# A one-core decoder layer: the order of weight loads, Silu, lambdas and banks, and a gate kept in SBUF

## The chip, the cores and the metric

The kernel runs on one core of a Trainium2 chip. The core has five engines that run side by side: TensorE (PE in the profile) multiplies matrices into PSUM, VectorE (DVE) and ScalarE (ACT) do elementwise work and are the ones that empty PSUM, GpSimd (POOL) does elementwise work in SBUF only, and SyncE (SP) does nothing but issue DMA transfers. ScalarE and GpSimd also issue a few. Each engine takes its instructions strictly in the order in which the program wrote them; between engines there are semaphores. The metric is device time in microseconds (us), less is better.

## The reference, cut to what matters

One layer, 512 tokens, width 1024, all in 32-bit floats:

```python
h = x @ w_in                                   # 1024 -> 9 x 1024
ua, va, za, qh, kh, vh, zb, ga, gb = split(h)
ya = gelu(ua) * spatial(layer_norm(gelu(va))) * silu(za)      # spatial: 8 groups, 128x128 lower triangular
lam = exp(sum(lam_q1 * lam_k1)) - exp(sum(lam_q2 * lam_k2)) + 0.2
o = diff_attention(rope(qh) / 8, rope(kh), vh, lam)           # 8 heads, 2 maps of 64, causal
yb = rms_norm(o) * 0.8 * silu(zb)
merged = sigmoid(ga) * (ya @ w_branch_a) + sigmoid(gb) * (yb @ w_branch_b)
ple = sigmoid(x @ w_ple_gate) * (p @ w_ple)                   # p: 512 x 256
x = layer_norm(2 ** 0.25 * x + merged @ w_out + ple)
```

The embedding's gate is `sigmoid(x @ w_ple_gate)`, called `pg` below; the lambdas are the scalars of `lam`.

## The kernel before

**Products.** Every fp32 matrix is split into a high part that TensorE reads in one pass (`wh`, made by a ScalarE copy) and a low part (`wl`, the rest, made by a VectorE subtraction). One matmul of the reference becomes three (`three`): high by high, high by low, low by high. Each of these 128x512 matmuls is a *product*, and `product` counts them. The count is the kernel's clock: `later(n, fn)` puts `fn` on an agenda, and it is written into the program as soon as n more products have been written. So "at product 14 of a unit" is a place in the program order of every engine that `fn` uses, not a time. The matmuls of attention and of the spatial products are not counted.

**Weights.** The weights are cut into units of 128x1024 (512 KB). `load(u)` has SP fetch unit u into one of three buffers `wr`; the buffer that unit u+3 needs is that of unit u, free once u is split. `spread(u)` writes the split: the high part two products later, the low part twelve. `next_unit` is called when TensorE starts unit u: it writes the loads up to u+5 and the split of u+3. A unit of q, k, zb, ua or za is 24 products long.

**Stages, in order.** 1. v from x (192 products, eight PSUM banks, `values_of_x`); the rope tables and `lam` are made on the side. While k, q and zb of the first head pair run, sums of quarters of x are made and stored (`sums_of_x`, issued from ScalarE). 2. Four rounds, one for each pair of heads p: `rope("k", p)`, `rope("q", p)`, `gate_b(p)`, each of two units. `rope` turns the banks with the tables, splits the result and has SP stack it by small copies (`stack`, L528; in round 0 half of them go by POOL), 24 products after the group; for k a pair of swapped copies per head follows 10 and 20 products later (`swap`, L539). `gate_b` has ScalarE empty two banks with Silu into `yb` (L560), `GATE` products after their last one. Attention of pair p-1 (`attention`) is spread over round p: its first score matmuls (L575) come at product 14 of the round. VectorE empties them (L580), ScalarE takes exponentials (L586), VectorE combines the two maps, TensorE transposes (L610), ScalarE copies them out (L612), TensorE multiplies by v (L621). There are three PSUM banks `pp` in turn for the units, two `sc` for scores, and `tr`, `po`, `tx`. 3. The rest of ua, and za. 4. Four `quad` stages, va, ga, gb, pg (x by w_ple_gate), 168 products each: a fast matrix product with seven products of quarters instead of eight. Weights of some steps are made by adding one unit onto another with an accumulating DMA from POOL (`follow`, L249). `keep` (L794) copies a bank out on ScalarE, `block` (L799) joins two pieces on VectorE, and `done` finishes a block 128x512. For ga, gb and pg `done` is `gate_done`: Sigmoid on ScalarE into a scratch tile (tag `t`, six buffers), and a store to DRAM by SP (L900). The spatial products (L875) read va and run in gb and in the first 40 products of pg. 5. `ple`: two units, 24 products each, p by w_ple into four banks each; `embed` (L935) multiplies each bank on VectorE by the gate, fetched from DRAM by `load_gate`, into `base`. 6. wb and wa (192 products each), out, and the last layer norm, which uses `lg` and `lb`.

PSUM sets for stages of eight banks are `main_banks()` (three `pp` and `tx`) and `other_banks()` (two `sc`, `tr`, `po`). wb writes the other banks first:

```python
    for c in range(2):
        banks = main_banks() if c else other_banks()
```

A tile with a tag takes the memory of the tile that had the tag before; the first write waits for the last use of the old one. `va`, and later `base`, have the tag V.

Of the kernel before, what the change touches and what calls it, by code (L numbers as in the profile page):

```python
# [12 lines left out]
F32 = mybir.dt.float32  # L13
# [3 lines left out]
AF = mybir.ActivationFunctionType  # L17
OP = mybir.AluOpType
AX = mybir.AxisListType

P = 128
D = 1024
T = 512
KT = D // P
NT = T // P
# [8 lines left out]


WARM = 9
GATE = 1
HIGH = (2,)
LOW = (12,)
ROPE = (2, 6, 8, 14, 18, 24)  # L40
# [121 lines left out]
def bcast(ap, n, parts=P):  # L162
    return bass.AP(tensor=ap.tensor, offset=ap.offset, ap=[[0, parts], [1, n]])
# [3 lines left out]
def hybrid_layer(ctx: ExitStack, tc: tile.TileContext, a, out: bass.AP):  # L167
    nc = tc.nc
    pe, dve, act, pool, sp = nc.tensor, nc.vector, nc.scalar, nc.gpsimd, nc.sync
# [7 lines left out]
    dram = ctx.enter_context(tc.tile_pool(name="dram", bufs=1, space=bass.MemoryType.DRAM))  # L177

    def pbank(tag, bufs):
        return psum.tile([P, T], F32, tag=tag, name=f"ps_{tag}", bufs=bufs)  # L180

    def pp():
        return pbank("pp", 3)

    def main_banks():
        return [pp(), pp(), pp(), pbank("tx", 1)]

    def other_banks():
        return [pbank("sc", 2), pbank("sc", 2), pbank("tr", 1), pbank("po", 1)]
# [5 lines left out]
    def later(n, fn, *args):  # L195

        clock[1] += 1
        heapq.heappush(agenda, (clock[0] + n, clock[1], fn, args))
# [30 lines left out]
    def load(u, pieces=1):  # L229
        if u >= len(STEPS) or u in raw or STEPS[u][3] is not None:  # L230
            return
        _, unit, chain, _ = STEPS[u]
        if chain == "a":
            if not sums:
                return
            r = sums[0].tile([P, 1024], F32, name="wa", tag="wa", bufs=3)
        else:
            r = wraw.tile([P, 1024], F32, name="wr", tag="wr")
        n = 1024 // pieces
        raw[u] = r  # L240
        for j in range(pieces):
            sp.dma_start(out=r[:, j * n:(j + 1) * n], in_=W[unit][:, j * n:(j + 1) * n])
            yield

    def follow(u):

        if u in FOLLOWS:
            raw[FOLLOWS[u]] = raw[u]
            pool.dma_start(out=raw[u], in_=W[STEPS[FOLLOWS[u]][1]], accum_op=OP.add)  # L249

    def parts_of(u):
        h = wsp.tile([P, 1024], F32R, name="wh", tag="wh")
        l = wsp.tile([P, 1024], F32R, name="wl", tag="wl")
        split[u] = (h, l)
        return h, l

    def prep(u, pieces=1):
        if u < len(STEPS) and u not in split:
            run(load(u))
            h, l = parts_of(u)  # L260
            n = 1024 // pieces
            for j in range(pieces):
                s = slice(j * n, (j + 1) * n)
                cut(h[:, s], l[:, s], raw[u][:, s])
                yield
            follow(u)

    def spread(u, high=HIGH[0], low=LOW[0]):

        if u >= len(STEPS) or u in split:  # L270
            return
        h, l = parts_of(u)

        def high_part():
            act.activation(h, raw[u], AF.Copy)  # L275

        def low_part():
            dve.tensor_tensor(out=l, in0=raw[u], in1=h.bitcast(F32), op=OP.subtract)  # L278
            follow(u)

        later(high, high_part)
        later(low, low_part)

    def next_unit(name):
        u = cursor[0]
        assert STEPS[u][0] == name, (STEPS[u][0], name)
        cursor[0] += 1
        for g in (prep(u), prep(u + 1), prep(u + 2), load(u + 3), load(u + 4), load(u + 5)):
            run(g)
        spread(u + 3)  # L290
        return split.pop(u)

    def next_pair(name):
# [21 lines left out]
    def run(gen):  # L315
        for _ in gen:
            pass

    def feature_group(ps, name, mh, ml):
        h, l = next_unit(name)  # L320
        for k in range(KT):
            s = slice(k * P, (k + 1) * P)
            three(ps, h[:, s], l[:, s], mh[:, k, :], ml[:, k, :], k == 0, k == KT - 1)
# [28 lines left out]
    for k in range(KT):  # L352
# [3 lines left out]
        if k < 2:  # L356
# [9 lines left out]
                       base=0, pattern=[[-1, P]], channel_multiplier=1)  # L366
# [186 lines left out]
    def gate_b(p):  # L553
# [7 lines left out]

        later(GATE, out_of)

# [112 lines left out]
                later(n + d, fn, h)  # L676

    rope_tables()
    later(150, lam)
    values_of_x()  # L680
    sums_of_x()
    ua = big.tile([P, KT, T], F32, name="ua", tag="U")
# [47 lines left out]
    post = ctx.enter_context(tc.tile_pool(name="post", bufs=1))  # L730
    sums.append(post)

    def tmp(name):
        return post.tile([P, T], F32, name=name, tag="t", bufs=6)
# [49 lines left out]
    def quad(name, turn, place, done, last=None):  # L784


        pair = [pp(), pp()], [pp(), pbank("tx", 1)]
        X, Y = pair if turn else pair[::-1]
        Z = [pbank("sc", 2) for _ in range(2)]
        kept = {}  # L790

        def keep(key, bank):
            kept[key] = tmp(key[0])
            act.activation(kept[key], bank, AF.Copy)  # L794

        def block(c, t, first, second, op, spare):
            z = place(c, t)
            z = spare if z is None else z
            dve.tensor_tensor(out=z, in0=first, in1=second, op=op)  # L799
            later(2, done, c, t, z, z)  # L800

        def after1(t):
            keep(("s1", t), Y[t])

        def after2(t):
            s1 = kept.pop(("s1", t))
            block(0, t, X[t], s1, OP.add, s1)

        def after5(t):
            keep(("s5", t), Z[t])  # L810

        def after6(t):
            keep(("s2", t), Y[t])
            later(2, block_of_6, t)

        def block_of_6(t):
            s2 = kept.pop(("s2", t))
            block(1, t, Z[t], s2, OP.subtract, s2)

        def after7(t):  # L820
            s5 = kept.pop(("s5", t))
            block(1, 2 + t, s5, Y[t], OP.subtract, s5)

        def after4(t):
            z = place(0, 2 + t)
            done(0, 2 + t, tmp("z") if z is None else z, Y[t])

        steps = ((X11, Y, True, after1), (X12, X, True, after2), (XS1, Z, True, after5),
                 (XN4, Z, False, None), (XS2, Y, False, after6), (XS3, Y, False, after7),
                 (X22, Y, False, after4))  # L830
        for i, (x, bank, first, after) in enumerate(steps):
            w = next_pair(name)
            if i == 6 and last:
                last()
            for t in range(2):
                for k in range(4):
                    h, l = w[k // 2]
                    m = slice((k % 2) * T, (k % 2 + 1) * T)
                    three(bank[t], *x(t, k), h[:, m], l[:, m], first and k == 0, k == 3, True)
                if after:  # L840
                    later(1, after, t)
# [50 lines left out]
        later(SPATIAL[0] + SPATIAL[1] * g, spatial, g)  # L892


    gates = {n: dram.tile([NT, 2, P, T], F32, name=f"gate_{n}") for n in ("ga", "gb", "pg")}

    def gate_done(name):
        def done(c, t, z, source):
            act.activation(z, source, AF.Sigmoid)
            sp.dma_start(out=gates[name][t, c], in_=z)  # L900

        return done
# [18 lines left out]
            later(40 + 12 * k, cut, phl[0][:, 0, k, :], phl[0][:, 1, k, :], pt)  # L921

    later(64, load_p)
    quad("pg", False, lambda c, t: None, gate_done("pg"), begin_ya)


    base = post.tile([P, NT, D], F32, name="base", tag="V")
    gate = {}

    def load_gate(name, c, t):  # L930
        gate[name, c, t] = tmp("gate")
        sp.dma_start(out=gate[name, c, t], in_=gates[name][t, c])

    def embed(c, t, bank):
        dve.tensor_tensor(out=base[:, t, c * T:(c + 1) * T], in0=bank, in1=gate.pop(("pg", c, t)), op=OP.mult)  # L935

    def residue(c, t):
        z = base[:, t, c * T:(c + 1) * T]
# [8 lines left out]
    def cut_yb(g):  # L947
        cut(ybh[:, g, :], ybl[:, g, :], yb[:, g, :])

    banks = other_banks(), main_banks()  # L950
    for t in range(NT):
        load_gate("pg", 1, t)
    for g in range(KT):
        later(4 + 12 * g, cut_yb, g)
    for c in (1, 0):
        h, l = next_unit("ple")
        for t in range(NT):
            ts = slice(t * P, (t + 1) * P)
            for k in range(2):
                m = slice(k * T, (k + 1) * T)  # L960
                three(banks[c][t], phl[0][:, 0, k, ts], phl[0][:, 1, k, ts], h[:, m], l[:, m], k == 0, k == 1)
            later(1, embed, c, t, banks[c][t])
            if c:
                later(4, load_gate, "pg", 0, t)


    lg = post.tile([P, D], F32, name="lg", tag="g")
    lb = post.tile([P, D], F32, name="lb", tag="b")
    pool.dma_start(out=lg, in_=bcast(a["ln_g"], D))
    pool.dma_start(out=lb, in_=bcast(a["ln_b"], D))  # L970

    mb = big.tile([P, NT, D], F32, name="mb", tag="Y")

# [7 lines left out]
    for c in range(2):  # L981
        banks = main_banks() if c else other_banks()
# [25 lines left out]
    for c in range(2):  # L1008
        banks = main_banks() if c else other_banks()
# [37 lines left out]
    banks = other_banks()  # L1047
# [4 lines left out]
    for t in range(NT):  # L1052
        ts = slice(t * P, (t + 1) * P)
        n = T if t < NT - 1 else T // 2
        for j in range(T // n):
            bank = pp()
# [50 lines left out]
```

## Time and profile before

| | us |
|---|---|
| median of 3 runs | 651.64 (651.27 to 652.54) |
| profiled execution, its own time | 649.57 |
| span of its trace, first to last instruction | 647.9 |
| TensorE busy in it | 629.4 |
| VectorE, ScalarE, GpSimd busy | 411.2, 298.8, 135.7 |
| DMA moved | 112.62 MB |

The granted clock of TensorE is 0.996 of full speed over the span. In the profile, L with a number is a line of the kernel. A row of the timeline is: start, length, engine, line, operation, what it writes and reads, shapes, how many in a row were merged (x4), and in brackets the idle time before it and what ended that. A `q` behind an engine's name is its sequencer (SPq: DMA issues of SP; the length is that of issuing, not of the transfer). Names like `ps_pp` are PSUM banks, `wr`, `wh`, `wl` a raw weight and its parts, `wa` a raw weight of a quad's chain. A matmul's row shows 0.39 us, but matmuls overlap.

### The profile page before, as it was taken

The numbers are of one execution on the slowest core, as the hardware profiler recorded it, in microseconds if no ns is written. First come the engines' busy times: TensorE is split into PE (matmuls) and PEld (weight loads), VectorE is DVE, ScalarE is ACT, GpSimd is POOL, SyncE is SP. The second block draws the span as 40 slices with busy tenths as digits, with TensorE's granted clock in tenths as the row PEclk, the third lists the DMA queues.
The fourth block names the chain that finished last, engine by engine and source line by source line (L and its number), as shares of the span: only waits on it lengthen the run. The fifth ranks groups of instructions, "written<-read, shape, count | busy, mean of one in ns | idle before, by whom it ended". The sixth has DMA issues, their size and how long they took to land.

```text
span 647.9 us, 8418 instructions
## 1 busy us (share of the span) xinstructions
PE 629.4 (97%) x2977; PEld 518.3 (80%) x2977; DVE 411.2 (63%) x720; ACT 298.8 (46%) x481; POOL 135.7 (21%) x135
## 2 busy tenths in 40 slices
PE   9999989999999999999999999999999999999994
PEld 6887867888888888888888886788878688888884
DVE  5548838868859856634335777777556657265367
ACT  6236345474464475573255655455455332122210
POOL 0001833325426502221112240321210000000023
PEclk9999999999999999999999999999999999999998
DMA  8527782752742742211999788898898656425003
GB/s 318 160 65 235 227 282 86 189 154 60 196 136 69 191 131 98 65 66 38 330 378 196 195 191 231 211 211 224 231 264 323 215 187 214 163 72 188 33 1 129
DMA packets 42795, 112.62 MB, mean 174 GB/s; under 512 B 6913, under 2 KB 6913, under 8 KB 42753
## 3 DMA queue, kind: packets, MB, share of 16 engines
q1 hardware_dynamic: 35040, 89.02, 41.8%
q0 software_dynamic: 5408, 18.88, 14.9%
q10 hardware_dynamic: 2304, 4.20, 1.8%
q8 instruction: 23, 0.38, 0.3%
q14 instruction: 20, 0.16, 0.1%
HBM read 86.90 MB, written 12.58 MB: 154 GB/s over the span
## 4 chain that ended last, share of the span: by engine, by line
issue 40%; PE 31%; DMA 10%; DVE 7%; POOL 6%; ACT 5%; SPq 0%; DVEq 0%; POOLq 0%; ACTq 0%
PE ps_pp L201 21%; DMA wa<-in_w 6%; PE ps_po L621 2%; PE ps_sc L575 2%; DVE wl L278 2%; POOL wa L249 1%; PE ps_sc L201 1%; ACT wh L275 1%; PE ps_tr L610 1%; DMA wr<-in_w 1%; DMA xsd<-at 1%; POOL rs L848 1%; DVE base L1044 1%; PE ps_tx L201 1%; PE ps_tr L201 1%
## 5 line engine op out<-in xcount | busy, mean ns | idle before, releaser
L278 DVE TENSOR_TENSOR wl<-wr,wh 128x1024 fp32r<-128x1024 f32 x94 | 121.5, 1297 | 83.7 <-ACT wh L275 81.8
L275 ACT ACTIVATE wh<-wr 128x1024 fp32r<-128x1024 f32 x94 | 98.5, 1056 | 131.0 <-PE ps_po L201 39.9
L201 PE MATMUL ps_pp<-xh,wh 128*128 128x512 f32 x320 | 128.5, 402 | 0.5 <-ACT v L442 0.5
L201 PE MATMUL ps_pp<-xl,wh 128*128 128x512 f32 x320 | 126.5, 395 | 0.0
L201 PE MATMUL ps_pp<-xh,wl 128*128 128x512 f32 x320 | 125.9, 393 | 0.0
L201 PEld LDWEIGHTS ps_pp<-xh,wh 128*128 128x128 f32 x320 | 60.2, 188 | 11.4 <-ACT v L442 0.9
L201 PEld LDWEIGHTS ps_pp<-xh,wl 128*128 128x128 f32 x320 | 60.1, 188 | 11.3
L201 PEld LDWEIGHTS ps_pp<-xl,wh 128*128 128x128 f32 x320 | 60.3, 188 | 11.1
L586 ACT ACTIVATE p<-p,st 128x128 f32<-128x128 f32 (+3 forms) x64 | 35.5, 556 | 49.9 <-DVE st L584 49.8
L278 DVE TENSOR_TENSOR wl<-wa,wh 128x1024 fp32r<-128x1024 f32 x32 | 38.8, 1222 | 20.8 <-ACT wh L275 20.6
L848 POOL TENSOR_TENSOR rs<-mv,mhalf 128x1 f32<-128x1 f32 x8 | 9.7, 1207 | 170.7 <-DVE mv L846 170.7
L249 POOL DMA_DIRECT2D wa<-in_w x24 | 21.0, 873 | 113.1 <-DVE wl L278 96.8
L201 PE MATMUL ps_pp<-wh,xh 128*128 128x512 f32 x96 | 37.8, 393 | 1.1 <-DVE s L799 1.1
L580 DVE CUSTOM_DVE_ANT_0 p<-ps_sc,mask 128x128 f32<-128x128 f32 (+3 forms) x64 | 31.0, 484 | 11.4 <-PE ps_sc L575 11.4
L201 PE MATMUL ps_pp<-wl,xh 128*128 128x512 f32 x96 | 37.5, 391 | 0.2 <-DVE wl L225 0.2
L201 PE MATMUL ps_pp<-wh,xl 128*128 128x512 f32 x96 | 37.4, 389 | 0.0
L275 ACT ACTIVATE wh<-wa 128x1024 fp32r<-128x1024 f32 x32 | 33.1, 1053 | 8.2 <-DMA wa<-in_w 8.1
L505 POOL TENSOR_TENSOR m<-m 128x512 f32<-128x512 f32 x8 | 10.7, 1333 | 103.6 <-DVE m L502 81.2
L621 PEld LDWEIGHTS ps_po<-v,at 128*128 128x128 f32 x160 | 22.3, 190 | 5.5 <-ACT at L612 3.3
L201 PE MATMUL ps_sc<-wl,xsh 128*128 128x512 f32 x64 | 25.1, 392 | 0.6 <-DVE wl L278 0.6
L201 PE MATMUL ps_sc<-wh,xsh 128*128 128x512 f32 x64 | 25.0, 391 | 0.0
L201 PE MATMUL ps_sc<-wh,xsl 128*128 128x512 f32 x64 | 24.9, 389 | 0.0
(318 smaller groups left out, 1333.6 us busy)
## 6 DMA issues: line engine op xcount, KB each, us to landing
wr<-in_w SPq DMA_DIRECT2D x88, 512.0 KB, 4.3
wa<-in_w POOLq DMA_DIRECT2D x24, 512.0 KB, 7.9
kx<-k SPq DMA_DIRECT2D x16, 256.0 KB, 6.0
wa<-in_w SPq DMA_DIRECT2D x8, 512.0 KB, 4.5
wr<-in_w POOLq DMA_DIRECT2D x8, 512.0 KB, 8.3
xr<-in_xT SPq DMA_DIRECT2D x8, 256.0 KB, 6.0
xsd<-p ACTq DMA_DIRECT2D x8, 256.0 KB, 3.8
xsd<-at ACTq DMA_DIRECT2D x8, 256.0 KB, 4.1
```

The lines of the kernel that those rows point to most:

```text
L201: pe.matmul(ps, s, m, start=start, stop=stop, skip_group_check=read_within)
L249: pool.dma_start(out=raw[u], in_=W[STEPS[FOLLOWS[u]][1]], accum_op=OP.add)
L275: act.activation(h, raw[u], AF.Copy)
L278: dve.tensor_tensor(out=l, in0=raw[u], in1=h.bitcast(F32), op=OP.subtract)
L505: pool.tensor_tensor(out=m[0], in0=m[0], in1=m[3], op=OP.subtract)
L575: pe.matmul(sc[m][:, :N], q[:, m, i * P:(i + 1) * P], kk[:, m, :N], start=o == 0, stop=o == 1)
L580: dve.tensor_tensor_reduce(out=pr[m][:, :n], in0=sc[m][:, :n], in1=mask[:, T - n:], scale=-(DK ** -0.5), scalar=3e38, op0=OP.add, op1=OP.m ...
L586: act.activation(pr[m][:, :n], pr[m][:, :n], AF.Exp, bias=st[:, m:m + 1], scale=-1.0, accum_out=st[:, 2 + m:3 + m])
L610: pe.transpose(tr[:, j * P:(j + 1) * P], ad[:, j * P:(j + 1) * P], ident)
L621: pe.matmul(po[:, i * P:(i + 1) * P], at[:, j * P:(j + 1) * P], v[:, j, h * P:(h + 1) * P], start=j == 0, stop=j == i)
L848: pool.tensor_tensor(out=rs, in0=mv[:, 1:2], in1=mhalf[:, 0:1], op=OP.pow)
L1044: dve.scalar_tensor_tensor(out=z, in0=z, scalar=rs[:, 0:1], in1=lb[:, c], op0=OP.mult, op1=OP.add)
```

## The change

Six edits, all in one diff:

- after the start of each unit of k, q and zb, at its product 14 (`ASK`), the load of unit u+6 is written, which otherwise comes with the next unit's start;
- the Silu of `gate_b` comes 6 products after the bank's last one instead of 1 (`GATE`);
- `lam` comes at product 144 instead of 150;
- the embedding's gate is no longer stored to DRAM: `base` is allocated ahead of the pg quad, the quad's blocks are written into it, Sigmoid works in place, and `embed` multiplies in place;
- `ple` uses the main banks and the other banks the other way round: its first unit (c = 1) now fills the other banks, its second (c = 0) the main ones;
- `lg` and `lb` are fetched by SP, 240 and 270 products after `ple`, instead of by POOL right behind it.

```diff
-GATE = 1
+GATE = 6
+ASK = 14
+EARLY_ASK = ("k", "q", "zb")
...
         for g in (prep(u), prep(u + 1), prep(u + 2), load(u + 3), load(u + 4), load(u + 5)):
             run(g)
         spread(u + 3)
+        if name in EARLY_ASK:
+            later(ASK, lambda: run(load(u + 6)))
         return split.pop(u)
...
-    later(150, lam)
+    later(144, lam)
...
-    gates = {n: dram.tile([NT, 2, P, T], F32, name=f"gate_{n}") for n in ("ga", "gb", "pg")}
+    gates = {n: dram.tile([NT, 2, P, T], F32, name=f"gate_{n}") for n in ("ga", "gb")}
...
-    quad("pg", False, lambda c, t: None, gate_done("pg"), begin_ya)
-
-
     base = post.tile([P, NT, D], F32, name="base", tag="V")
+
+    def embedding_gate(c, t, z, source):
+        act.activation(z, source, AF.Sigmoid)
+
+    quad("pg", False, lambda c, t: base[:, t, c * T:(c + 1) * T], embedding_gate, begin_ya)
...
     def embed(c, t, bank):
-        dve.tensor_tensor(out=base[:, t, c * T:(c + 1) * T], in0=bank, in1=gate.pop(("pg", c, t)), op=OP.mult)
+        z = base[:, t, c * T:(c + 1) * T]
+        dve.tensor_tensor(out=z, in0=bank, in1=z, op=OP.mult)
...
-    banks = other_banks(), main_banks()
-    for t in range(NT):
-        load_gate("pg", 1, t)
+    banks = main_banks(), other_banks()
...
             later(1, embed, c, t, banks[c][t])
-            if c:
-                later(4, load_gate, "pg", 0, t)
...
-    pool.dma_start(out=lg, in_=bcast(a["ln_g"], D))
-    pool.dma_start(out=lb, in_=bcast(a["ln_b"], D))
+    later(240, sp.dma_start, lg, bcast(a["ln_g"], D))
+    later(270, sp.dma_start, lb, bcast(a["ln_b"], D))
```

## The prediction

> **What bounds the kernel now.** I read the page first, then the waits of TensorE, then the timeline of TensorE around each of those waits, and from there the queue that held each one up.
>
> ```profile
> PE 629.4 (97%) x2977; PEld 518.3 (80%) x2977; DVE 411.2 (63%) x720; ACT 298.8 (46%) x481; POOL 135.7 (21%) x135
> ```
>
> ```profile
> PE ps_pp L201 <- ACT s L794: 1.6, 2, 1.1
> PE ps_po L621 <- ACT at L612: 0.7, 3, 0.2
> ```
>
> TensorE is busy for 97% of the span, and the change adds and removes no matmul. So only TensorE's gaps can be won, and a new cost counts only if it opens a gap. The second fence shows waits by cause: total, count, longest. The timeline of TensorE gives the gaps that the change touches (start, length, what, idle time and its releaser):
>
> ```profile
> 48.77 0.39 PE L201 MATMUL ps_po<-wl,xh 128*128 128x512 f32 x1
> 49.00 0.39 PE L201 MATMUL ps_po<-wh,xl 128*128 128x512 f32 x1
> 49.87 0.50 PE L201 MATMUL ps_pp<-xh,wh 128*128 128x512 f32 x1 [0.48 <-ACT v L442]
> 50.21 0.40 PE L201 MATMUL ps_pp<-xl,wh 128*128 128x512 f32 x1
> ...
> 94.67 0.39 PE L201 MATMUL ps_pp<-xh,wl 128*128 128x512 f32 x1
> 97.95 0.39 PE L575 MATMUL ps_sc<-k,q 128*128 128x256 f32 x1 [2.89 <-DVE st L580]
> ...
> 137.85 0.39 PE L201 MATMUL ps_pp<-xh,wl 128*128 128x512 f32 x1
> 138.47 0.71 PE L621 MATMUL ps_po<-v,at 128*128 128x128 f32 x4 [0.23 <-ACT at L612]
> ...
> 478.71 0.39 PE L201 MATMUL ps_pp<-wh,xsl 128*128 128x512 f32 x1
> 480.18 0.50 PE L201 MATMUL ps_pp<-wh,xsh 128*128 128x512 f32 x1 [1.09 <-ACT s L794]
> ...
> 503.06 0.40 PE L201 MATMUL ps_sc<-wh,ybl 128*128 128x512 f32 x1
> 504.16 0.50 PE L201 MATMUL ps_sc<-wh,ybh 128*128 128x512 f32 x1 [0.70 <-DVE base L935]
> 504.73 0.40 PE L201 MATMUL ps_sc<-wh,ybl 128*128 128x512 f32 x1
> 505.36 0.50 PE L201 MATMUL ps_tr<-wh,ybh 128*128 128x512 f32 x1 [0.23 <-DVE base L935]
> 505.92 0.40 PE L201 MATMUL ps_tr<-wh,ybl 128*128 128x512 f32 x1
> 506.44 0.50 PE L201 MATMUL ps_po<-wh,ybh 128*128 128x512 f32 x1
> ```
>
> A matmul lasts 0.39 us but the next one starts 0.23 us later (48.77 to 49.00), so I measure a gap as start to start, less 0.23. That gives 0.64 us at 49, 3.05 at 95, 0.39 at 138, 1.24 at 479, and 0.87, 0.40 and 0.29 at 503 to 506. After a gap the next step is also longer: 49.87 to 50.21 is 0.34, 0.11 too much.
>
> **The change part by part.** "Product" is one step of the kernel's own count, 0.23 us.
>
> *Lambdas at product 144 instead of 150.* ScalarE's exponential and its table load now stand in front of two weight splits rather than behind them; in the old order they are the last thing before the copies of v out of PSUM, which release the bank that TensorE wants at 49.87. The same instructions run six products earlier. The second split keeps its own wait (for TensorE's use of the old weight buffer) and leaves the copies nothing to wait for after it. I take the whole gap: 0.64 + 0.11 = 0.75. Bounds: 0 if that second split is still the last to end, 0.75 if not.
>
> *Weights of k, q and zb asked at product 14 of a unit instead of at the next unit's start (24).* 24 loads move; each passes, on SP's queue, whatever is issued in between: the copies that stack k or q, or one pair of swapped-key copies. The 3.05 us gap is the place where it matters:
>
> ```profile
> 73.35 1.25 SPq L242 DMA_DIRECT2D wr<-in_w  x1
> ...
> 82.07 0.34 SPq L242 DMA_DIRECT2D wr<-in_w  x1
> ...
> 91.73 6.31 SPq L242 DMA_DIRECT2D wr<-in_w  x4
> ```
>
> ```profile
> 91.39 0.35 PE L575 MATMUL ps_sc<-k,q 128*128 128x256 f32 x1
> ```
>
> ```profile
> 95.37 1.06 ACT L275 ACTIVATE wh<-wr 128x1024 fp32r<-128x1024 f32 x1 [5.45 <-DMA wr<-in_w]
> ```
>
> ```profile
> 96.46 1.22 DVE L278 TENSOR_TENSOR wl<-wr,wh 128x1024 fp32r<-128x1024 f32 x1 [5.76 <-ACT wh L275]
> 97.60 0.28 DVE L580 CUSTOM_DVE_ANT_0 p<-ps_sc,mask 128x128 f32<-128x128 f32 x1
> ```
>
> Between 82.07 and 91.73 SP issues the copies of q. The weight issued at 91.73 is split on ScalarE at 95.37, its low part on VectorE at 96.46, and only behind that does VectorE empty the first scores (97.60), which TensorE needs to go on at 97.95. Asked early, this load goes out in front of the q copies, near 82, so it lands near where the load of 82.07 was used. The gap of 3.05 + 0.11 goes. What is late next is the first score matmul itself, at 91.39, which reads those q copies. The DMA load there is (columns: busy time by engine, clock, DMA share, GB/s):
>
> ```profile
> 66.00:72.00 6.00, 6.00 (x29) 4.95 (x28) 5.30 (x6) 2.64 (x4) 6.00 (x7) 1.00 0.53 145
> 72.00:82.00 10.00, 10.00 (x46) 8.28 (x45) 7.54 (x10) 3.68 (x6) 7.32 (x8) 1.00 1.00 304
> ```
>
> From 72 on the DMA engines are full. One weight tile (0.52 MB) at 304 GB/s is 1.72 us. One load enters the full stretch before the q copies (that of 91.73) but one leaves it too: the load of 73.35 moves in front of the k copies, into the half-empty 66 to 72. So I take the q copies to land when they do now. TensorE arrives 0.75 sooner (lambdas), and waits those 0.75 there: net 3.16 - 0.75 = 2.41. Bounds: 3.16 if the copies also come 0.75 sooner; 3.16 - 0.75 - 1.72 = 0.69 if the extra tile pushes them.
> [...]
>
> In the other three attention stages no gap comes from weights, so the early loads win nothing there. Their cost is on SP's queue: each waits for VectorE to free its buffer, with the copies behind it.
>
> ```profile
> 124.62 1.21 DVE L278 TENSOR_TENSOR wl<-wr,wh 128x1024 fp32r<-128x1024 f32 x1
> ```
>
> ```profile
> 128.69 2.67 SPq L528 DMA_DIRECT2D q<-l  x4
> ```
>
> ```profile
> 139.71 0.28 PE L575 MATMUL ps_sc<-k,q 128*128 128x256 f32 x1
> ```
>
> Head 0's last q copies are issued by 131.36 and used at 139.71: 8.35 us. The buffer is freed at 125.83, before those copies begin, so the load costs them its issue time, under 1 us. I take 0.
>
> *Silu 5 products later.* At the turn of each attention stage ScalarE runs this:
>
> ```profile
> 134.72 1.28 ACT L560 ACT_TABLE_LOAD   x1
> 136.01 1.09 ACT L560 ACTIVATE yb<-ps_pp 128x512 f32<-128x512 f32 x2
> 136.98 1.06 ACT L275 ACTIVATE wh<-wr 128x1024 fp32r<-128x1024 f32 x1
> 137.93 0.49 ACT L612 ACTIVATE at<-ps_tr 128x384 f32<-128x384 f32 x1
> ```
>
> The copy at 137.93 is what TensorE waits for at 138.47, and it comes two products after Silu in the old order, three before it in the new. It moves up by 1.28 + 1.09 = 2.4 us, more than the gap, so 0.39 goes in each of three stages: 1.17. (The waits give 0.7 of idle time for the three; start to start holds the refill too.) What is late next: the two gate banks come free some 2.5 us later, but the group that writes them again begins 24 products (5.5 us) after the old Silu. If that cover were gone it would cost up to 2.4 a stage. The number of table loads stays.
>
> *The embedding's gate stays in SBUF.* Eight stores and eight loads of 256 KB leave SP's queue and the DMA engines; the eight sigmoids and eight multiplications stay. It bears on the gap at 479:
>
> ```profile
> 476.13 1.06 ACT L275 ACTIVATE wh<-wr 128x1024 fp32r<-128x1024 f32 x1 [5.38 <-DMA wr<-in_w]
> ...
> 478.59 1.06 ACT L275 ACTIVATE wh<-wr 128x1024 fp32r<-128x1024 f32 x1 [0.88 <-DMA wr<-in_w]
> ```
>
> ScalarE waits for two added-up weights, and the copy that TensorE needs stands behind the second. Two stores of 256 KB issued before them go (at 304 GB/s some 1.7 us of DMA time), and SP, no longer held for sigmoids, issues its next loads before the added-up weights instead of beside them. 1.7 is more than 1.24, so the gap goes: 1.24 + 0.11 = 1.35. Bounds 0 and 1.35. The multiplications also lose their wait for the gate's loads.
> New: `base` takes va's memory before the last two spatial products have read va, and its first block is written by VectorE three products before the last of them is issued.
>
> ```profile
> 459.24 0.69 DVE L799 TENSOR_TENSOR s<-ps_pp,s 128x512 f32<-128x512 f32 x1
> ```
>
> ```profile
> 459.90 1.05 PE L875 MATMUL ps_tr<-aux,va 128*128 128x128 f32 x8
> ```
>
> That write must then wait from 459.24 to 460.95, 1.7 us; behind it stand the weight split and the adds of VectorE, and the sigmoid on ScalarE. The splits it delays are wanted some 2 us later, so I charge 0.3 (an estimate); bounds 0 and 1.7.
>
> *Banks swapped.* The last four embedding banks were the ones that wb writes first; VectorE empties each in 0.7 us while TensorE is already there. Now wb begins on the banks of the first half, done 24 products earlier. The three gaps go with their refills: 0.87 + 0.40 + 0.29 + 3 x 0.11 = 1.89. The old bound is 0, if VectorE were over 5 us behind; nothing behind it is that late. The second half's banks are wanted 96 products later.
>
> *lg and lb from SP at products 240 and 270.* Two issues leave POOL, two join SP amid wa, where TensorE shows no gap; they are used at the very end. 0; without SP's lead it would be their issue time, under 1 us each.
>
> **Sum.** 0.75 + 2.41 + 1.17 + 1.35 - 0.30 + 1.89 = 7.27 us. Against the profiled execution (649.57, that is the span of 647.9 and 1.7 around it) this gives 642.3. That execution lies 2.07 below the median of the runs, 651.64; taken off the median: 644.4 us.
>
> **The rivals.**
> (a) The early weight pushes the q copies: the lower bound of 0.69 instead of 2.41, so 644.4 + 1.7 = 646.1. For it: DMA share 1.00. Against it: the load that leaves. [...]
> (b) The gap at 479 stays, or moves to where VectorE now waits for va: 1.35 lost, up to 1.4 more paid: 645.8 to 647.2. For it: the added-up weights are issued on POOL behind those delayed splits. Against it: two stores gone.
> (c) The loads are asked sooner but held by their buffers, so the gap at 95 stays: 644.4 + 2.4 = 646.8. Against it: the load of 91.73 shows no wait of its own, it followed the q copies at once.
> (d) Slower: an early load that waits long for its buffer holds back the q copies of three attention stages. SP's own waits hold this row:
>
> ```profile
> SPq L242 <- DVE wl L278: 181.9, 45, 12.4
> ```
>
> The copies must land too: the weight issued at 91.73 was there 3.6 us later (95.37). So of the 8.35 us some 4.7 are to spare, and the longest wait, 12.4, in front of the q copies costs 7.7 a stage, 23 in three: 644.4 + 23 = 667. It turns the sign once the hold is over 4.7 + 7.27 / 3 = 7.1 us. Against it: 125.83 above.
>
> **How the numbers follow.** Likeliest (gain 6 to 9): 0.60. (a) 0.15, (b) 0.10, (c) 0.05; a change inside 0.2% 0.03, which is about what a measurement of this kernel can tell from none; (d) 0.07. All the upper bounds together are 0.75 + 3.16 + 1.17 + 1.35 + 1.89 = 8.3, so 643.3, and the three runs spread by 1.3: low 642.0. High: (a) and (b) together, 647.5. Faster 0.90, same 0.03, slower 0.07.
>
> **What would show it.** Right: no TensorE wait on st L580 near 95 but one of under 1 us at the first scores; no wait on L612; none on L935; the wait on L794 near 479 gone while that near 392 stays; SP with a weight load between the k and the q copies' issue. Wrong: L575 waiting for q copies, a VectorE wait for TensorE near 460 with a TensorE gap near 468, or SP's L528 waiting behind L242.

## The result, and the profile after

The changed kernel runs in 642.00 us, the median of four runs (641.43 to 643.05), against 652.09 us (651.27 to 652.85) for the kernel before beside it: a ratio of 0.9847, 95% interval 0.9828 to 0.9867, or 8.7 to 11.2 us gained. The profiled execution took 641.59 us, span 639.9 (before: 649.57 and 647.9). Line numbers moved: L201, L242, L275 and L278 of before are L203, L244, L277 and L280, and from L442 to L895 they are 4 higher (L560 is L564, L575 is L579, L612 is L616).

The page's line of busy time after:

```profile
PE 626.4 (98%) x2977; PEld 519.3 (81%) x2977; DVE 411.7 (64%) x720; ACT 299.1 (47%) x481; POOL 134.6 (21%) x133
```

TensorE still does the same 2977 matmuls; its share rose by a point because the span shrank. The waits of TensorE after, all of them (total, times, longest):

```profile
PE ps_pp L203 <- ACT yb L564: 1.5, 1, 1.5
PE ps_po L343 <- DVE zeros L340: 1.3, 1, 1.3
PE ps_sc L579 <- DMA q<-l: 0.8, 1, 0.8
PE ps_sc L203 <- DVE wl L280: 0.8, 1, 0.8
PE ps_pp L203 <- DVE s L803: 0.4, 1, 0.4
PE ps_pp L203 <- DVE wl L280: 0.2, 1, 0.2
```

Gone are the rows on the emptied scores (st, L580), on the copy L612, on v, on `base` and on the quads' copy (L794). New are the first, the third and the last. The first and the third lie where the 3 us gap was, on TensorE's timeline:

```profile
86.84 0.39 PE L203 MATMUL ps_pp<-xh,wl 128*128 128x512 f32 x1
88.76 0.50 PE L203 MATMUL ps_pp<-xh,wh 128*128 128x512 f32 x1 [1.53 <-ACT yb L564]
...
91.84 0.39 PE L203 MATMUL ps_pp<-xl,wh 128*128 128x512 f32 x1
93.01 0.36 PE L579 MATMUL ps_sc<-k,q 128*128 128x256 f32 x1 [0.78 <-DMA q<-l]
```

Measured start to start, less 0.23, as in the prediction, the two traces compare like this. The last column is how much earlier TensorE is behind the place, with the refill and what small rows lie around it:

| near (us) | what ends the gap | before | after | won |
|---|---|---|---|---|
| 49 | copies of v | 0.64 | none | 0.75 |
| 87 | Silu of round 0 | none | 1.69 | -1.84 |
| 92 | q copies, first scores | none | 0.94 | -0.85 |
| 95 | st, second scores | 3.05 | none | 3.37 |
| 138, 185, 231 | copy L612 | 0.39 each | none | 1.43 |
| 392, 398 | banks of the ga quad | 0.65, 1.24 | 0, 0.52 | 1.81 |
| 414 | weight split | 0.87 | 1.03 | -0.28 |
| 479 | copy L794, pg quad | 1.25 | none | 1.57 |
| 481 | weight split, pg quad | none | 0.39 | -0.5 |
| 503 to 506 | `base` | 0.87, 0.40, 0.29 | none | 2.14 |
| the first 5 us | | | | 0.23 |

That is 7.8 of the 8.0 us by which the spans differ; the rest lies behind the last matmul. The gaps of the ga quad are touched by no edit, and they vary without one: run again, the kernel before has the second of them at 1.23 and not the first, and each of the five kernels below that are built on the changed one has the second again, at 1.13 to 1.27.

Where the 1.69 comes from is on ScalarE's timeline of the changed kernel:

```profile
85.74 1.06 ACT L277 ACTIVATE wh<-wr 128x1024 fp32r<-128x1024 f32 x1 [2.19 <-DMA wr<-in_w]
86.81 1.28 ACT L564 ACT_TABLE_LOAD   x1
88.11 1.09 ACT L564 ACTIVATE yb<-ps_pp 128x512 f32<-128x512 f32 x2
```

Silu at product 6 stands behind a weight split that product 1 stood ahead of. In round 0 that split waits 2.19 us for its weight, Silu waits with it, and TensorE wants the gate's bank at 87. SP's timeline shows the weight's way:

```profile
65.58 0.33 SPq L244 DMA_DIRECT2D wr<-in_w  x1
...
76.35 1.85 SPq L244 DMA_DIRECT2D wr<-in_w  x1
78.37 1.42 SPq L543 DMA_DIRECT2D kx<-k  x2
79.90 2.52 SPq L244 DMA_DIRECT2D wr<-in_w  x1
82.92 1.52 SPq L532 DMA_DIRECT2D q<-h  x2
```

The weight issued at 76.35 is the one split at 85.74, over nine us later. The weight that used to follow the q copies (91.73) is issued at 79.90, ahead of them, as forecast. The last q copy of head 0 landed at 92.70, against 91.19 before: 1.51 later. That is not yet the price of the request, since this landing varies by as much without it (92.86 in the next run, which has no edit).

The block of `base` that had to wait for the spatial product does so, with no gap of TensorE at 468 (VectorE's timeline):

```profile
456.34 0.69 DVE L803 TENSOR_TENSOR base<-ps_pp,s 128x512 f32<-128x512 f32 x1 [1.66 <-PE ps_tr L879]
```

### The profile page after: what moved, and what is told of

Read it like the earlier page. It is cut to its first block, busy times and chain, and to the rows that moved or that the text cites. A ratio compares the mean times of both kernels' runs of the same rounds, so it can differ in the third digit from the quotient of the medians.

```text
span 639.9 us, 8392 instructions
## 1 busy us (share of the span) xinstructions
PE 626.4 (98%) x2977; PEld 519.3 (81%) x2977; DVE 411.7 (64%) x720; ACT 299.1 (47%) x481; POOL 134.6 (21%) x133
## 4 chain that ended last, share of the span: by engine, by line
PE 49%; issue 34%; DMA 7%; DVE 6%; ACT 2%; POOL 2%; DVEq 0%; POOLq 0%; ACTq 0%; SPq 0%
PE ps_pp L203 34%; DMA wa<-in_w 4%; PE ps_sc L579 3%; PE ps_sc L203 3%; PE ps_po L625 3%; PE ps_tx L203 2%; DMA wr<-in_w 1%; PE ps_tr L614 1%; DVE wl L280 1%; DMA q<-l 1%; ACT wh L277 1%; DVE base L1049 1%; POOL wa L251 1%; DVE p L479 1%; PE ps_tr L203 1%
## 5 line engine op out<-in xcount | busy, mean ns | idle before, releaser
L280 DVE TENSOR_TENSOR wl<-wr,wh 128x1024 fp32r<-128x1024 f32 x94 | 121.5, 1297 | 73.7 <-ACT wh L277 73.4
L277 ACT ACTIVATE wh<-wr 128x1024 fp32r<-128x1024 f32 x94 | 98.4, 1056 | 124.5 <-PE ps_po L203 32.7
L203 PE MATMUL ps_pp<-xh,wh 128*128 128x512 f32 x320 | 128.6, 402 | 1.5 <-ACT yb L564 1.5
L203 PE MATMUL ps_pp<-xl,wh 128*128 128x512 f32 x320 | 126.5, 395 | 0.0
L203 PE MATMUL ps_pp<-xh,wl 128*128 128x512 f32 x320 | 125.9, 394 | 0.0
L203 PEld LDWEIGHTS ps_pp<-xh,wh 128*128 128x128 f32 x320 | 60.2, 188 | 12.4 <-ACT yb L564 2.0
L203 PEld LDWEIGHTS ps_pp<-xh,wl 128*128 128x128 f32 x320 | 60.2, 188 | 11.3
L203 PEld LDWEIGHTS ps_pp<-xl,wh 128*128 128x128 f32 x320 | 60.3, 188 | 11.2
L280 DVE TENSOR_TENSOR wl<-wa,wh 128x1024 fp32r<-128x1024 f32 x32 | 38.9, 1223 | 21.6 <-ACT wh L277 21.5
L203 PE MATMUL ps_pp<-wh,xh 128*128 128x512 f32 x96 | 37.9, 395 | 0.4 <-DVE s L803 0.4
L203 PE MATMUL ps_pp<-wl,xh 128*128 128x512 f32 x96 | 37.6, 392 | 0.3 <-DVE wl L280 0.2
L277 ACT ACTIVATE wh<-wa 128x1024 fp32r<-128x1024 f32 x32 | 33.1, 1054 | 9.3 <-DMA wa<-in_w 9.0
L203 PE MATMUL ps_pp<-wh,xl 128*128 128x512 f32 x96 | 37.4, 389 | 0.0
L203 PE MATMUL ps_sc<-wl,xsh 128*128 128x512 f32 x64 | 25.1, 393 | 0.8 <-DVE wl L280 0.8
L203 PE MATMUL ps_sc<-wh,xsh 128*128 128x512 f32 x64 | 25.0, 391 | 0.0
L203 PE MATMUL ps_sc<-wh,xsl 128*128 128x512 f32 x64 | 24.9, 390 | 0.0
```

The costliest lines, as they stand in the source:

```text
L203: pe.matmul(ps, s, m, start=start, stop=stop, skip_group_check=read_within)
```

## The experiments

None of these kernels leaves out any of the computation. Ratios are to the kernel before, run beside them on the same chip.

### The kernel before once more

No edit.

> The kernel before, unchanged, as a second profile of it. Theory A (the difference of the two traces is the change): the ratio is 1.000, and TensorE's gaps stand as in the first profile: 3.05 us at the first head's second scores, 1.24 in the pg quad, and also 0.65 and 1.24 in the ga quad near 392 and 398, which are nearly gone in the trace after though no edit touches the ga quad. Theory B (the ga quad's gaps vary from execution to execution): the sum of those two gaps is off by over 0.7 us from the 1.9 of the first profile, while the 3.05 stays within 0.7.

652.55 us, ratio 1.0009 [0.9981, 1.0036]. Neither theory foresaw the largest difference, a wait for the q copies; the ga quad's gaps sum to 1.23 instead of 1.9, just short of what Theory B asks. The profiled span is 653.6, which is 5.7 above the span that the prediction worked from. Three of its waits, then four us at a time (length, busy time of PE, PEld, DVE, ACT, POOL, granted clock, DMA share, GB/s):

```profile
PE ps_sc L575 <- DVE st L580: 2.7, 1, 2.7
PE ps_sc L201 <- DVE base L935: 2.2, 2, 1.5
PE ps_sc L575 <- DMA q<-l: 1.8, 1, 1.8
```

```profile
96.00:100.00 4.00, 1.28 (x7) 0.66 (x5) 1.85 (x6) 2.73 (x4) 0.00 (x0) 0.97 0.68 271
100.00:104.00 4.00, 4.00 (x12) 3.24 (x13) 3.40 (x12) 2.53 (x9) 0.00 (x0) 0.60 0.37 131
```

This execution waits for the q copies too, before the change; the first one had no such wait, and the gaps at `base` are larger here. And the clock falls: 12 matmuls start from 100 to 104 us where the first trace of this kernel has 21. (0.03 + 0.40) x 4 us = 1.72 us of clock lost, what 3.4 us at half speed lose. Over its span the mean clock is 0.991, against 0.996 in the first trace: some 3.3 us in all, about twice that.

### The early request alone

```diff
+ASK = 14
+EARLY_ASK = ("k", "q", "zb")
...
+        if name in EARLY_ASK:
+            later(ASK, lambda: run(load(u + 6)))
```

> Only the early loads of k, q and zb. Theory A (the prediction: the weight leaves the gap, the q copies land as before): the 3.05 us gap at the second scores goes, the first scores start near 91.4 as before, gain 3.2 us, ratio 0.995. Theory B (the early weight pushes the q copies, as in the trace after): the first scores wait 1.5 us for the q copies, gain 1.5 us, ratio 0.9977.

650.74 us, ratio 0.9995 [0.997, 1.002]: no change that can be told from none. The gap on st is gone, and in its place stands

```profile
PE ps_sc L579 <- DMA q<-l: 1.6, 1, 1.6
```

SP issues its q copies from 87.05 on, behind the weight issued at 83.37; in the kernel before from 82.51. The weight does what the prediction says, and the wait for the copies takes most of it back. How much of that wait is the request's this run does not say: the kernel before, run once more, waits 1.8 us for them without it.

### Silu at product 6 alone

```diff
-GATE = 1
+GATE = 6
```

> Only Silu 6 products after the bank instead of 1. Theory A (the prediction): the three waits on the transposed copy go, 1.2 to 1.4 us won, nothing paid, ratio 0.998. Theory B (in round 0 Silu now stands behind a weight split that waits for its weight): the first k group of round 1 waits for the Silu of round 0, some 3 us here since that weight lands at 88.4; of these most are taken from the 3.05 us gap that follows, since that one ends when a weight lands, so the total is again 1.0 to 1.4 us won, but the gap at the second scores shrinks below 1 us and a wait on yb of 2 to 3.5 us stands ahead of it.

652.41 us, ratio 1.0005 [0.9978, 1.0033]. The three waits on L612 are gone. In round 0:

```profile
PE ps_pp L201 <- ACT yb L560: 4.9, 1, 4.9
```

```profile
89.87 1.06 ACT L275 ACTIVATE wh<-wr 128x1024 fp32r<-128x1024 f32 x1 [4.07 <-DMA wr<-in_w]
90.94 1.28 ACT L560 ACT_TABLE_LOAD   x1
92.24 1.08 ACT L560 ACTIVATE yb<-ps_pp 128x512 f32<-128x512 f32 x2
```

```profile
88.00:92.00 4.00, 0.00 (x0) 0.00 (x0) 1.04 (x1) 2.11 (x2) 0.00 (x0) 0.75 0.83 246
92.00:96.00 4.00, 3.11 (x7) 2.49 (x8) 0.18 (x1) 2.04 (x5) 0.00 (x0) 0.50 0.80 260
96.00:100.00 4.00, 4.00 (x19) 3.30 (x18) 2.04 (x7) 2.99 (x6) 0.00 (x0) 0.89 0.61 218
```

The same chain as after the whole change, with a weight that comes 4 us later still, and 4.9 us in which TensorE does nothing and its clock stands at half for some 6.9 us (1.00 + 2.00 + 0.44 us lost; what falls into the idle time costs nothing). The edit wins 1.2 us in three rounds and loses about as much in the first: no difference is measured.

### Lambdas alone

```diff
-    later(150, lam)
+    later(144, lam)
```

> Only the lambdas at product 144. Theory A (the prediction): the gap of 0.64 us at the start of k goes, 0.75 us won, ratio 0.9988. Theory B (the next wait ends when a weight lands, which does not come sooner): the gap at 49 goes but the gap at the second scores grows from 3.05 to 3.8 us, gain 0, ratio 1.000.

649.79 us, ratio 0.9976 [0.9955, 0.9998]. The gap at 49 is gone, 0.75 us, which is 0.0012 and lies in the interval. The waits for the q copies (0.83) and on st (2.55) are both there, and 1.72 us of clock is lost from 96 to 104 us.

### The gate on chip alone

```diff
+    base = post.tile([P, NT, D], F32, name="base", tag="V")
...
-    quad("pg", False, lambda c, t: None, gate_done("pg"), begin_ya)
+    quad("pg", False, lambda c, t: base[:, t, c * T:(c + 1) * T], embedding_gate, begin_ya)
```

> The kernel before, with only the embedding's gate kept on chip (banks, lg and lb as before). Theory A (the prediction): the gap of 0.6 to 1.25 us in the pg quad goes, and no gap takes its place near 468; the waits on the multiplication (L935, banks written last) stay, 1.5 to 2 us. Gain 1.3 us, ratio 0.998. Theory B (the write of the gate into the memory of va waits for the last spatial products and holds VectorE up): VectorE shows a wait of over 1 us for the spatial products near 460, and a TensorE gap of 0.3 to 1.5 us appears behind it in the same quad; gain 0 to 1 us.

648.92 us, ratio 0.9944 [0.9918, 0.997], 2.0 to 5.4 us. The gap at 479 is gone; a new one of 0.62 stands at 490, a weight split again, as the 0.39 after the whole change, and VectorE waits 1.66 us for the spatial products at 465: the two signs of Theory B. The gaps on `base` stay at 0.72 and 0.39. So the rows show some 0.7 won where 1.05 was forecast; the rest of the measured gain has no row in the one execution profiled and stays open. In the run of the kernel before above, the gaps on `base` were up to 1.66, when the gate still came from DRAM; whether late loads of it make the difference was not tried.

### Banks alone

```diff
-    banks = other_banks(), main_banks()
+    banks = main_banks(), other_banks()
```

> The kernel before, with only the two sets of banks of the embedding swapped; its gate still goes by DRAM. Theory A (the prediction: the gaps at 503 to 506 come from the order of the banks alone): they go, 1.9 us won, ratio 0.997, and the gap of the pg quad stays. Theory B (they come from the gate's way by DRAM too: the multiplications wait for its loads): half of them or more stay, or move to the second half of wb, under 1 us won.

649.17 us, ratio 0.9961 [0.9944, 0.9979], 1.4 to 3.7 us. All gaps on `base` are gone and nothing takes their place; the one near 479 stays at 0.77.

### The changed kernel, Silu of round 0 at product 1

```diff
-        later(GATE, out_of)
+        later(GATE if p else 1, out_of)
```

> The kernel after, with Silu at 1 product in round 0 alone and at 6 in the others. Theory A (the waits of round 0 add up): the wait of 1.7 us on yb before the first k group of round 1 goes and 1.7 us are won, ratio 0.982 to the kernel before. Theory B (they stand in a row in front of one landing, that of the q copies): the wait on yb goes but the wait for the q copies at the first scores grows from 0.9 to 2.6 us; nothing is won, ratio 0.9847 as after.

644.86 us (643.83 to 645.70), ratio 0.9879 [0.9858, 0.9899]: slower than the changed kernel. The wait for Silu is gone, and TensorE comes to the first scores that much sooner, to wait there for the same copies:

```profile
PE ps_sc L579 <- DMA q<-l: 3.1, 1, 3.1
```

1.72 us of clock is lost from 92 to 100 us (0.67 and 0.90). Two waits of 1.69 and 0.94 became one of 3.23, and the one cost more.

### The changed kernel, sums of x earlier

The pieces were begun during v, to take the stores of the sums of x (4 MB) out of 72 to 92 us.

```diff
-            later(8 + 14 * i, piece, i // 4, i % 4)
+            later(60 + 14 * i, piece, i // 4, i % 4)
...
-    values_of_x()
     sums_of_x()
+    values_of_x()
```

> The kernel after, with the sums of quarters of x and their stores (4 MB) made from product 60 on, while v is made, rather than from product 200 on, beside the copies of k and q. Theory B (what is left at the front of round 1 is DMA load: the stores share the engines with the weights and the q copies): the DMA share between 72 and 90 falls well below 1, both the wait on yb and the wait for the q copies go, 2 to 2.6 us won against after, ratio 0.981. Theory C (the queue order alone sets the landing, not the load): the q copies land as late as in after, nothing is won, ratio 0.985.

655.04 us, ratio 1.0033 [1.0016, 1.005]. Both waits near 90 are gone, but this does not show that the stores crowded that stretch: TensorE comes to the first scores 10 us later (103.36 instead of 93.01), and the DMA share ahead of them, from 90 to 98 us, is still 1.01. What the time shows is that the pieces pushed the sines and the copies of v back on ScalarE:

```profile
PE ps_pp L203 <- ACT v L446: 10.9, 1, 10.9
```

```profile
59.63 1.57 ACT L446 ACTIVATE v<-ps_pp 128x512 f32<-128x512 f32 x3 [1.13 <-DVE at L489]
```

### The changed kernel without the early request

```diff
-EARLY_ASK = ("k", "q", "zb")
+EARLY_ASK = ()
```

> The changed kernel without the early request; all the other parts stay. Theory A (the request is worth more beside the later Silu than alone, since it brings the weight whose split stands ahead of the first round's Silu): that Silu waits as long as with the later Silu alone, some 4.9 us instead of 1.69 near 87, no wait for q copies at the first scores (0.94 in the changed kernel), none at the second scores, and a stall of that length brings one or two windows of half clock of 3.41 us, at 1.7 us each: 642.0 + 4.9 - 1.69 - 0.94 + 1.7 to 3.4 = 646.0 to 647.7 us. Theory B (it is worth nothing, as alone, 650.74 against 651.73): 642.0 us, with the gap before the second scores back in place of the wait for q copies.

645.96 us (645.02 to 649.53), ratio 0.9913 [0.9886, 0.994]; the span is 4.3 above that of the changed kernel. Theory A, with a shorter wait (3.1 instead of 4.9):

```profile
PE ps_pp L203 <- ACT yb L564: 3.1, 1, 3.1
```

```profile
88.00:92.00 4.00, 1.64 (x4) 1.35 (x5) 1.22 (x1) 3.25 (x5) 0.00 (x0) 0.71 0.41 103
92.00:96.00 4.00, 4.00 (x11) 3.11 (x10) 0.52 (x1) 1.59 (x2) 0.00 (x0) 0.50 0.96 357
```

The weight in front of Silu is now issued at 80.03 instead of 76.35. From 92 to 96 us eleven matmuls start, half of the usual, while nothing makes TensorE wait. So the request, which alone showed no gain, is worth some 4 us beside the later Silu: without it that edit makes a stall of 3.25 us, and the clock stood at 0.50 behind it (3.4 us lost).

### Second head's swapped k copies later

Are the transfers under way what delays the weight and the q copies? The same edit in three kernels: the changed one, the changed one with Silu of round 0 at product 1, and the kernel before.

```diff
-                    later(10 + 10 * hd, swap, 2 * p + hd)
+                    later(10 + (10 if p else 60) * hd, swap, 2 * p + hd)
```

> The changed kernel with the swapped k copies of the second head (two transfers of 256 KB) asked for 50 products later, in round 0 alone. Theory A (the weights and the q copies of 72 to 92 us land late because too much is under way at once): 0.5 MB less at some 250 GB/s is 2 us, so the weight that landed at 85.66 lands near 84 and the last q copy of the first head near 91: the wait for the Silu (1.69) shrinks to 0.3 to 0.8, that for q copies (0.94) goes, and the time is 639.8 to 640.6 us. Theory B (the order on SP's queue sets them, or the sums' stores take the room that comes free): both waits stay within 0.4 us, 642 us.

640.61 us (640.52 to 641.85), ratio 0.9824 [0.9796, 0.9853], 1.4 us below the changed kernel, though the intervals of the two ratios overlap. In the trace it is Theory A, and better than it said: neither wait near 90 is left. SP's and ScalarE's timelines:

```profile
74.76 2.27 SPq L543 DMA_DIRECT2D kx<-k  x2
77.14 2.86 SPq L244 DMA_DIRECT2D wr<-in_w  x2
80.08 1.22 SPq L532 DMA_DIRECT2D q<-h  x2
...
90.30 1.14 SPq L543 DMA_DIRECT2D kx<-k  x2
```

```profile
84.50 1.06 ACT L277 ACTIVATE wh<-wr 128x1024 fp32r<-128x1024 f32 x1 [0.64 <-DMA wr<-in_w]
85.58 1.28 ACT L564 ACT_TABLE_LOAD   x1
86.87 1.09 ACT L564 ACTIVATE yb<-ps_pp 128x512 f32<-128x512 f32 x2
```

The last q copy of head 0 landed at 88.81, 3.9 us sooner: 0.5 MB less stands in front of the copies, and SP issues them from 80.08 instead of 82.92. The weight in front of Silu landed at 84.41, 1.25 us sooner though issued 0.8 later. That this comes of the edit is not shown: the moved copies stood behind this weight on SP's queue, and with Silu of round 0 early, without this edit, it landed at 84.67.

> The changed kernel with the second head's swapped k copies later, as in the run before this one, and the first round's Silu at one product after its bank instead of six. Theory A (transfers, as there): the wait for the Silu is gone as in the run with the first round's Silu early (644.86), and the wait for q copies, 3.1 us in that run, is shortened by the 2 us of the 0.5 MB to about 1.1, under the length at which the clock halved: 642.0 - 1.69 + 0.2 = 640.5 us. Theory B: the wait for q copies stays near 3 us, with a window of half clock, 644 to 645 us.

640.01 us (639.54 to 640.41), ratio 0.9811 [0.9778, 0.9844], the fastest kernel here, though its interval and that of the one above overlap. All of its TensorE waits:

```profile
PE ps_po L343 <- DVE zeros L340: 1.3, 1, 1.3
PE ps_pp L203 <- DVE s L803: 1.0, 1, 1.0
PE ps_sc L203 <- DVE wl L280: 0.7, 1, 0.7
```

Early Silu, which lost 2.9 us against the changed kernel, loses nothing once the q copies are there (they landed at 91.08, against 93.17 with early Silu and the old place of the swapped copies).

> The kernel before with one edit: the second head's swapped k copies 50 products later in round 0. The weight that ended the 3.05 us gap before the second scores was asked for at 91.73, behind the q copies on SP's queue, and landed at 95.35; with two transfers of 256 KB fewer ahead it is asked for and lands some 2 us earlier, so the gap shrinks to about 1 us. Theory A (the clock carries the part of the gain that the two traces do not show): with no stall over 2 us near 95 there is no window of half clock there either, which cost 0 to 3.4 us an execution, about 2 us at the median: 652 - 2.0 - 2.0 = 648 us, granted clock 1.00 from 92 to 104 us. Theory B (the clock has nothing to do with the length of the stall): the windows of half clock stay, 650 us. Theory C (the weight comes no sooner, being behind what waits for the sums' stores): 652 us with the gap of 3 us in place.

650.02 us (646.35 to 652.71), ratio 0.9973 [0.9954, 0.9993]. The profiled execution is as Theory A has it, 646.35, no clock lost near 95, and the stall short:

```profile
PE ps_sc L575 <- DVE st L580: 0.8, 1, 0.8
```

It is the fastest of twelve, though, and the median is Theory B's number. The mean clock, listed with each execution, has a median of 0.995 here and 0.993 in the 17 executions of the kernel before beside it (0.994 in all 79): that is 0.6 to 1.3 us, not the 2 expected. What stalled in the other eleven is not recorded.

## Why the prediction was right, and where its sum was not

The direction, the time (644.4, range 642.0 to 647.5) and most places were right; the median came out at the lower edge of the range, the gain at 10.1 instead of 7.27 us. Term by term:

- Lambdas, 0.75: 0.75 in the two traces, and the same gap goes with this edit alone.
- Early request and Silu in round 0, 2.41: the step that failed is "I take the q copies to land when they do now". They landed 1.51 later in this pair of traces, close to the 1.72 of rival (a). How much of that the request causes one pair cannot say. With the old order of loads the last copy landed at 90.29 to 92.86 in seven traces (92.86 in the kernel before run again, 90.29 in the changed kernel without the request), with the early request at 92.70, 93.17 and 93.37. So later copies do go with the request, by some 1.2 us in the mean, and "now" was one execution of several. The request alone and the early Silu show the copies' wait at its full length, 1.81 and 3.23 us. With the 1.84 of Silu the three rows of round 0 give 3.37 - 1.84 - 0.85 = 0.68, the lower bound (0.69) by another sum.
- Silu, 1.17: 1.43 in three rounds, by the mechanism named. The step that failed is "What is late next": it priced the banks by the product count (24 products of cover) and did not look at what ScalarE would have to do ahead of Silu in its new place. In round 0 that is a split with a late weight. The trace of before held the rows (ScalarE's timeline):

```profile
86.32 1.09 ACT L560 ACTIVATE yb<-ps_pp 128x512 f32<-128x512 f32 x2
88.38 1.06 ACT L275 ACTIVATE wh<-wr 128x1024 fp32r<-128x1024 f32 x1 [0.98 <-DMA wr<-in_w]
```

  The split behind Silu waits for its weight; Silu, moved behind it, waits too. Alone, the cover was gone by 4.9 us, twice the "up to 2.4" given.
- Gate on chip, 1.35 - 0.30 = 1.05: 1.57 - 0.5 = 1.07. The write of `base` waits 1.66, as forecast 1.7, but nothing comes of it near 468; the loss is a weight split 25 us later. Whether the one leads to the other the traces do not show.
- Banks, 1.89: 2.14; alone 1.4 to 3.7.
- lg and lb, 0: no row of TensorE names them; not run alone.
- Gap near 392 "stays": in this execution it went, with part of that at 398. In the runs of the kernel before or of one edit, 392 shows 0 to 2.6 us. 1.81 of the 8.0 is such variation.

So the forecast mechanisms gave 0.75 + 0.68 + 1.43 + 1.07 + 2.14 = 6.1, 1.2 less than the sum. What made the gain 10 all the same was not in the sum at all, and that it carried the time from 646.0 (652.1 less 6.1) to the other edge of the range and not past it is luck. 2.0 are the ga gaps and the start, which differ from execution to execution. The other 2 us or so is that the execution of before behind the prediction lies under the others: 649.57 against a median of 652.09. It had no wait for q copies, which the kernel before run again, lambdas, gate and banks alone (all with the old order of loads) show at 1.95, 0.83, 0.78 and 1.46 us. And it lost no clock near 95, while those four each lost 1.72 us there. "Taken off the median" assumed that the gaps of one execution stand for all. The mean clock listed with each execution bears the second point out: 0.994 at the median of the 79 executions of the kernel before beside the experiments (0.996 in the one of the prediction), 0.997 in the changed kernel's four. Executions of the kernel before at 0.997 have a median of 650.4 us (7 of them), those at 0.993 one of 652.9 (24); 0.004 of 629 us of matmuls is 2.5 us, the whole difference. Between these ends the relation is loose: 651.9 at 0.994, 651.7 at 0.995 and at 0.996. Against the clock as the whole answer speaks also the swap in the kernel before, where one stall shrank and the median clock rose by 0.001 to 0.002 only.

Of the signs named ahead, these held: no wait on st, none on L612, none on `base`, none on L794 near 479, a weight load between the copies of k and of q, a first-score wait under 1 us (0.94). The wrong sign "L575 waiting for q copies" held as well: the prediction listed the same row under both, so it told nothing. Two other wrong signs held in part and cost TensorE nothing that the traces show: VectorE's wait near 460 without the gap at 468, and SP's stacking copies behind a weight, up to 1.6 us in each later round (up to 1.0 before). The lower bound charged the q copies with the whole of a weight ahead on SP's queue, 1.72 us, an estimate from 0.52 MB at 304 GB/s. The traces agree in direction: with two 256 KB transfers fewer ahead on SP's queue the last q copy of head 0 lands 3.9 us sooner in the changed kernel, 2.1 with early Silu and 2.9 in the kernel before. That is more than the 1.72 us of that estimate, and the 1.51 us of a weight ahead lie within the spread between executions.

## What to carry to other kernels

Moving an instruction later in an engine's program order means reading what then stands in front of it, in every round, with the wait of each (2.19 us for the split ahead of Silu in round 0); counting the slack of its readers is not enough. What stood ahead on SP's queue in the full stretch (DMA share 1.00 from 72 to 82 us) was paid by the q copies issued behind it: two swapped copies cost them 2.1 to 3.9 us here. So look first for a transfer in such a stretch that nobody needs soon and move that: here neither wait of round 0 was left in the trace. And one trace of before is one draw: profile it again before gaps of a DMA-bound stretch are added up, and test an edit in the company it will have: the request, which alone showed no gain, was worth some 4 us beside the later Silu.

## What was unexpected of the hardware

Some stalls of TensorE cost more than their length. Behind gaps the granted clock stood at 0.5 for some 3.4, 6.9 or 10.2 us, twice the clock lost: 1.72 us lost from 92 to 104 us in five executions (the kernel before again, lambdas, gate, banks, and early Silu), 3.44 with Silu alone, 3.4 without the request, 5.12 from 52 to 64 us around the stall of 10.9 us with the sums earlier. What falls while TensorE idles costs nothing; the rest does: with Silu alone the matmuls from 93.48 to 96.04 us, at a clock of 0.50, start 0.43 us apart, and those from 96.88 on 0.23.

No length of a gap parts these executions from the others: gaps of 0.78 and then 1.82 us (gate alone) lost 1.72 us of clock, 1.69 and then 0.94 (the changed kernel) none, a single 3.05 (the kernel before, first trace) none, a single 3.23 (early Silu) 1.72, single ones of 3.25 (without the request) and 5.07 (Silu alone) 3.4. Here are the rows of that first trace of the kernel before around its gap of 3.05 us, at full clock throughout (columns as above):

```profile
92.00:96.00 4.00, 3.06 (x14) 2.19 (x13) 0.00 (x0) 0.63 (x1) 0.00 (x0) 1.00 0.84 285
96.00:100.00 4.00, 2.05 (x10) 1.68 (x11) 2.78 (x11) 3.55 (x7) 0.00 (x0) 1.00 0.62 208
100.00:104.00 4.00, 4.00 (x21) 3.35 (x20) 3.93 (x13) 1.26 (x5) 0.00 (x0) 1.00 0.12 48
```

So whether a gap cost clock is read from the granted clock of its own execution, not from the gap. What decides it the runs do not show: none of them varied the gap alone.
